# First stage of a two-layer trunk: modulation blocks loaded ahead of token groups 2 and 3, and the product groups put into another order

## The chip, the core and the metric

The kernel runs on one core of one Trainium2 chip. The metric is the device time of one execution in microseconds (us). Before the change, three runs took 1563.63, 1566.26 and 1572.01 us; the median is 1566.26 us.

## What is computed

The reference is one step of a two-layer trunk with 1024 latent tokens and 128 context tokens of width 1024. The change touches only the start of layer 0: the modulation, the pre-norm, and the key and value columns of the input product.

```python
def rms_norm(x, g):
    y = xf * lax.rsqrt(jnp.mean(xf * xf, axis=-1, keepdims=True) + EPS)
    return y * g
def adaln(cond, w, b):
    m = (jax.nn.silu(cond) @ w + b)[:, None, :]      # w: 1024 x 3072
    return split_last(m, (D_MODEL, D_MODEL, D_MODEL))  # shift, scale, gate
def pre_norm(x, g, mod):
    shift, scale, _ = mod
    return rms_norm(x, g) * (1 + scale) + shift
# even layer: q, k, v, ga, ub, gb = split(pre_norm(x) @ w_in); here only k and v (256 columns)
```

Everything behind it (attention, pooling, the second layer, the outputs) is as it was.

## The kernel before

The 1152 tokens are nine tiles of 128 (eight latent, the last one context), and each tile is loaded as 128 x 1024 (`xn`, 512 KB). Three tiles make a token group g = 0, 1, 2. The 1024 features are eight blocks k of 128.

A **product group** (k, g) is feature block k for token group g. Its work has two parts. `pn(k, g)` transposes the three normalised tiles on TensorE (three `tp` matmuls into one PSUM buffer), applies scale and shift on VectorE (`hf`; two instructions for g = 2, because the context tokens have other constants), rounds to the high part on ScalarE (`hTh`), and takes the low part on GpSimd (`hTl`). `kvg(k, ...)` then does nine matmuls of 128x256 (`kv`): high by high, low weights by high, high by low for three tiles. All 24 product groups add into five PSUM accumulators. The list `seq` is the order of the product groups, and `kvq(i)` does the matmuls of entry i.

The scale and shift of feature blocks 2b and 2b+1 come from **modulation block** b = 0 to 3. `mod_block_load(b)` loads four weight tiles `wmb` (512 KB each), `mod_block(b)` does 64 small matmuls into `modps` and copies the result out on VectorE (`mrow`), and `mod_block_end(b)` transposes it on TensorE and makes `sh` and `sc` with three short VectorE operations. So `pn(k, g)` needs the normalised tiles of g and modulation block k // 2.

Normalising a tile is a square-and-sum (`sqx`) and a square root (`xd`) on ScalarE, and a reciprocal (`xr`) and a scaling (`xn`) on VectorE. `norm_x` does the four in a row for one tile; `norm_x1` and `norm_x2` split them.

The weights of the k and v columns come in two halves (`raw`), each split into `whi` (ScalarE) and `wlo` (VectorE): `kv.load1(0)` and `kv.split1(0, ...)` for blocks 0 to 3, `kv.load1(1)` and `kv.split1(1, ...)` for blocks 4 to 7. `zeros(n)` are matmuls of zeros into the accumulators; they add nothing to a result and keep TensorE at work.

The order is written by hand: every engine works off its instructions in the order of the code, and an instruction that waits holds all behind it on its engine. All loads go through one queue on SyncE, in code order. The buffer for `hf` exists twice, and three PSUM buffers are left for `tp` and `modps` beside the accumulators. The 17 general slots of the pool that `wmb`, `raw`, `whi`, `wlo` and `zero` share are used in turn.

Names of lines: L115 every matmul, L124 every transpose, L131 ScalarE copies and casts (`hTh`, `whi`), L136 VectorE copies (`mrow`), L139 VectorE two-operand operations (`sh`, `sc`, `wlo`), L142 the same on GpSimd (`hTl`), L149 `xn`, L151 `hf`, L156 and L158 `xd` and `xr`, L337 and L589 `sqx`.

Of the kernel before, what the change touches and what calls it, by code (L numbers as in the profile page):

```python
# [566 lines left out]
def layer0(kn):  # L567
# [9 lines left out]
    def load_x(t):  # L577
        xn[t] = kn.S([128, 1024], name="xn")
        kn.dma(xn[t], xin(t))

    def norm_x(t):
        kn.xnorm(xn[t], kn.T([128, 1024], tag="sqx", bufs=1), xn[t])
# [3 lines left out]
    def norm_x1(t):  # L586

        ss = rx[t] = kn.T([128, 1], tag="xss3", bufs=3)
        nc.scalar.activation(out=kn.T([128, 1024], tag="sqx", bufs=1), in_=xn[t], func=AF.Square, accum_out=ss)  # L589

    def norm_x2(t):
        kn.vts(xn[t], xn[t], kn.rstd(rx[t], D, [128, 1], "x"))

    kv = Chunk(kn, w_in[:, 512:768], 256)
    mb = {}
# [4 lines left out]
    mb[0] = kn.mod_block_load(0)  # L600
    kv.load1(0)
    kn.setup1()
    for t in range(3, 6):
        load_x(t)
    mb[1] = kn.mod_block_load(1)
    for t in range(6, 9):
        load_x(t)
    kv.load1(1)

    hTh = [kn.S([128, 1152], F32R, name=f"hTh{k}") for k in range(8)]  # L610
    hTl = [kn.S([128, 1152], F32R, name=f"hTl{k}") for k in range(8)]
# [7 lines left out]
    def zeros(n, st=True, sp=True):  # L619
        for i in range(n):  # L620
            kn.mm(acc[i % 5], zero[:, 0:128], zero, st, sp)
# [4 lines left out]
    def pn(k, g, b=None):  # L626
        c = slice(384 * g, 384 * g + 384)
        kn.prenorm_k(0, g, k, xn[3 * g:3 * g + 3], hTh[k][:, c], hTl[k][:, c], b=b)

    def kvg(k, ts):  # L630
        for i in range(3):
            for t in ts:
                c = slice(128 * t, 128 * t + 128)
                last = i == 2 and k == 7 and (t == 8 or t % 2 == 1)
                kn.mm(kvps(t), (hTl if i == 2 else hTh)[k][:, c], (kv.lo if i == 1 else kv.hi)(k), False, last)


    seq = [(0, 0), (1, 0), (0, 1), (1, 1), (2, 0), (3, 0), (2, 1), (3, 1), (0, 2), (1, 2), (2, 2), (3, 2)]
    seq += [(k, g) for q in (4, 6) for g in range(3) for k in (q, q + 1)]
    kvq = lambda i: kvg(seq[i][0], range(3 * seq[i][1], 3 * seq[i][1] + 3))  # L640
    zeros(8)
    kn.setup()
# [11 lines left out]
    m = kn.mod_block(0, mb.pop(0))  # L654
    kn.mod_block_end(*m)
    zeros(10, False, False)
    kv.split1(0, True, 1)
    for t in range(3, 5):
        norm_x1(t)
    for k in range(2):  # L660
        pn(k, 0, tps[k])
    norm_x1(5)
    kv.split1(0, True, 2)
    mb[2] = kn.mod_block_load(2)
    for t in range(3, 6):
        norm_x2(t)
    for i in range(2):
        kvq(i)
    zeros(3, False, False)
    for i in range(2, 4):  # L670
        pn(*seq[i])
        zeros(3, False, False)
    for t in range(6, 9):
        norm_x(t)
    for i in range(2, 4):
        kvq(i)
    m = kn.mod_block(1, mb.pop(1))
    kn.mod_block_end(*m)
    for i in range(4, 7):
        pn(*seq[i])  # L680
    kv.split1(1, True)
    mb[3] = kn.mod_block_load(3)
    wl = Stream([Chunk(kn, w_in[:, 0:256], 256, veng=True), Chunk(kn, w_in[:, 256:512], 256, veng=True)])

    rt = {}
# [12 lines left out]
    kn.dma(cs[:, 1], I["k_sina"].rearrange("(t p) d -> p t d", p=128))  # L698
    kn.dma(nw[:, 2], I["cache_a_k"][0, 0])
    wl._load(0)  # L700
    for i in range(4, 24):
        if i in (8, 14):
            m = kn.mod_block(2 + i // 14, mb.pop(2 + i // 14))
        if i in (9, 15):
            kn.mod_block_end(*m)
        if i + 3 < 24:
            pn(*seq[i + 3])
        if i == 21:
            for c, w in rt.values():
                for x in range(2):  # L710
                    kn.ptt(c[:, x], cs[:, x], w[:, x, None, :].to_broadcast([128, 8, 64]))
        if i == 21:
            wl.need(0)
            wl._load(1)
        kvq(i)
# [1596 lines left out]
def body(nc, tc, I, O):  # L2312
    with ExitStack() as es:
        with tc.manual_schedule():
            kn = Kern(nc, tc, I, O, es)
            units, Qs, KHp, KLp, Vp = layer0(kn)
            attention_A(kn, units, Qs, KHp, KLp, Vp)
# [75 lines left out]
```

## Time and profile before

| what | value |
|---|---|
| median of three runs | 1566.26 us (1563.63 to 1572.01) |
| time of the profiled execution | 1571.76 us |
| its span | 1570.0 us |
| mean granted TensorE clock | 0.984 |
| TensorE busy | 1510.9 us (96%) |
| VectorE / ScalarE / GpSimd busy | 51% / 42% / 39% |
| last `kv` matmul begins | 67.96 us |

The profile comes from one execution, whose own time is 5.50 us over the median. TensorE is abbreviated PE (PEld is its weight load), VectorE DVE, ScalarE ACT, GpSimd POOL, SyncE SP. A row of the timeline gives start and length in us, the engine, line and operation, the tiles written and read, the count, and in square brackets the idle time before the instruction and what ended it. The rows of stretches give, for each engine, busy us in the stretch and instructions, then the granted clock (PEclk), the share of the DMA engines and GB/s.

### The profile page before, as it was taken

The page shows a single profiled execution, that of the slowest core. Times are in us where ns is not written, and L with a number is a line of the kernel's source. Part 1 is how long each engine was busy: PE and PEld are TensorE (multiplying, and loading weights), DVE is VectorE, ACT ScalarE, POOL GpSimd, SP SyncE. Part 2 cuts the span into 40 slices and gives each one's busy share as a digit, 9 for nine tenths or more (in the row PEclk, how much of TensorE's full clock was granted, in tenths as well). Part 3 has the DMA queues.
Part 4 walks back from the last instruction along what each step waited for, and adds up shares of the span by engine and source line. Part 5 has one row for each costly group of instructions (what it writes and reads, how often), then busy time and mean ns, then how long its engine had stood idle before and what let it go on. Part 6 is the DMA issues. An engine that isn't in the chain of part 4 may idle for free.

```text
span 1570.0 us, 23369 instructions
## 1 busy us (share of the span) xinstructions
PE 1510.9 (96%) x8957; PEld 1231.8 (78%) x8957; DVE 803.6 (51%) x1788; ACT 655.4 (42%) x1402; POOL 606.6 (39%) x508
## 2 busy tenths in 40 slices
PE   8998999999999999999999999999999999999998
PEld 6987998955545688998999999999866666665786
DVE  4575232466687655634353544423755555445643
ACT  5323212265645323444454545444454344345211
POOL 2652212069778224440313122001166566565221
PEclk9999999999999999999999999999999999899999
DMA  9343104120001232411304041050000000023241
GB/s 346 97 171 124 41 28 141 50 92 14 1 14 54 81 107 71 81 44 36 65 16 100 16 76 39 22 159 1 19 1 28 8 27 15 21 61 111 96 143 54
DMA packets 114079, 104.80 MB, mean 67 GB/s; under 512 B 41776, under 2 KB 99952, under 8 KB 113968
## 3 DMA queue, kind: packets, MB, share of 16 engines
q1 hardware_dynamic: 113792, 103.23, 22.1%
q8 instruction: 71, 1.16, 0.3%
q14 instruction: 40, 0.33, 0.1%
q10 hardware_dynamic: 176, 0.07, 0.0%
HBM read 87.54 MB, written 15.75 MB: 66 GB/s over the span
## 4 chain that ended last, share of the span: by engine, by line
PE 81%; DVE 9%; ACT 5%; DMA 2%; issue 2%; POOL 1%; SPq 0%; DVEq 0%; ACTq 0%; POOLq 0%
PE cg L115 14%; PE yps L115 12%; PE st L115 10%; PE gate L115 9%; PE pv L115 9%; PE lat L115 4%; PE mp L115 4%; PE cpv L115 3%; PE cS L115 2%; PE cT L124 2%; PE dq L115 2%; DVE mx L989 2%; DMA raw<-in_w_in_e 1%; PE kv L115 1%; PE dv L115 1%
## 5 line engine op out<-in xcount | busy, mean ns | idle before, releaser
L989 DVE TENSOR_REDUCE mx<-mp 128x1 f32<-128x384 f32 x384 | 190.1, 547 | 106.6 <-PE mp L115 105.3
L142 POOL TENSOR_TENSOR acc<-acc,P 128x1024 f32<-128x1024 f32 x84 | 200.6, 2388 | 67.4 <-ACT P L1029 64.5
L1029 ACT ACTIVATE P<-st 128x512 f32<-128x512 f32 x256 | 148.4, 598 | 151.4 <-PE st L115 137.3
L115 PE MATMUL yps<-whi,ohl 128*128 128x512 f32 x576 | 182.9, 393 | 0.0
L115 PE MATMUL cg<-hT1h,whi 128*128 128x384 f32 x480 | 169.2, 352 | 0.3 <-DVE hf L151 0.3
L115 PE MATMUL cg<-hT1h,wlo 128*128 128x384 f32 x480 | 161.9, 337 | 0.0
L115 PE MATMUL cg<-hT1l,whi 128*128 128x384 f32 x480 | 161.5, 337 | 0.0
L142 POOL TENSOR_TENSOR wlo<-raw,whi 128x1024 fp32r<-128x1024 f32 x25 | 60.0, 2400 | 245.8 <-ACT whi L131 174.4
L115 PEld LDWEIGHTS yps<-whi,ohl 128*128 128x128 f32 x576 | 108.1, 188 | 25.8 <-issue 3.7
L115 PE MATMUL yps<-wlo,ohl 128*128 128x512 f32 x288 | 112.2, 389 | 0.0
L115 PE MATMUL gate<-hTh,whi 128*128 128x384 f32 x288 | 98.9, 343 | 3.7 <-ACT whi L131 3.7
L115 PE MATMUL gate<-hTh,wlo 128*128 128x384 f32 x288 | 98.1, 340 | 0.3 <-DVE wlo L139 0.3
L115 PE MATMUL gate<-hTl,whi 128*128 128x384 f32 x288 | 97.6, 339 | 0.0
L115 PEld LDWEIGHTS cg<-hT1h,whi 128*128 128x128 f32 x480 | 90.5, 188 | 4.9 <-issue 3.4
L1638 ACT ACTIVATE cs<-cs,cnm 128x640 f32<-128x640 f32 (+1 forms) x64 | 54.8, 857 | 93.4 <-DVE cnm L149 92.7
L115 PEld LDWEIGHTS cg<-hT1l,whi 128*128 128x128 f32 x480 | 90.6, 189 | 0.5
L115 PEld LDWEIGHTS cg<-hT1h,wlo 128*128 128x128 f32 x480 | 90.1, 188 | 0.0
L139 DVE TENSOR_TENSOR wlo<-raw,whi 128x1024 fp32r<-128x1024 f32 (+2 forms) x35 | 46.6, 1340 | 65.3 <-ACT whi L131 64.6
L115 PE MATMUL pv<-P,dV 128*64 128x512 f32 x288 | 74.6, 646 | 1.7 <-DVE mx L989 1.7
L131 ACT CAST whi<-raw 128x1024 fp32r<-128x1024 f32 (+2 forms) x60 | 62.0, 1038 | 27.7 <-DMA raw<-in_w_in_e 13.5
L115 PE MATMUL st<-QH,dKh 96*128 96x512 f32 x144 | 63.5, 441 | 2.2 <-ACT P L1029 2.2
L115 PE MATMUL mp<-KH,QP 128*128 128x384 f32 x192 | 59.2, 365 | 6.4 <-DVE mx L989 3.5
(427 smaller groups left out, 3526.0 us busy)
## 6 DMA issues: line engine op xcount, KB each, us to landing
raw<-in_w_in_o SPq DMA_DIRECT2D x20, 512.0 KB, 4.1
raw<-in_w_in_e SPq DMA_DIRECT2D x18, 512.0 KB, 7.5
wmb<-in_w_mod SPq DMA_DIRECT2D x16, 512.0 KB, 8.5
wm<-in_w_mod SPq DMA_DIRECT2D x16, 512.0 KB, 7.4
wg<-in_w_mod SPq DMA_DIRECT2D x16, 512.0 KB, 5.2
x<-xr SPq DMA_DIRECT2D x9, 512.0 KB, 2.8
xr<-x SPq DMA_DIRECT2D x9, 512.0 KB, 4.6
xn<-in_x_sample SPq DMA_DIRECT2D x8, 512.0 KB, 7.1
```

Source lines behind the costliest of these rows:

```text
L115: self.nc.tensor.matmul(out=out, lhsT=l, rhs=r, start=st, stop=sp)
L124: self.nc.tensor.transpose(out, in_, self.ident[0:n, 0:n])
L131: self.nc.scalar.copy(out=out, in_=in_)
L139: self.nc.vector.tensor_tensor(out=out, in0=a, in1=b, op=op)
L142: self.nc.gpsimd.tensor_tensor(out=out, in0=a, in1=b, op=op)
L989: kn.nc.vector.tensor_reduce(out=self.mx[:, h, t, c:c + 1], in_=b, axis=AX.X, op=ALU.max)
L1029: kn.nc.scalar.activation(out=P[:, h], in_=a, func=AF.Exp, scale=self.scale)
L1638: nc.scalar.activation(out=s[:, 0:n], in_=s[:, 0:n], func=AF.Exp, bias=nm, accum_out=sm)
```

## The change

The loads are put in another order: modulation block 1 ahead of tiles 3 to 5, modulation block 2 and the second half of the k and v weights ahead of tiles 6 to 8, modulation block 3 last. The product groups are put in another order: blocks 0 to 3 of g = 0, blocks 0 to 3 of g = 1, then blocks 4 and 5 of both, then six blocks of g = 2, then blocks 6 and 7. Modulation block 1 is worked off right behind the first two product groups. The normalisation of tiles 3 to 5 is written behind it, and that of tiles 6 to 8 directly ahead of the first product group with g = 2. The count of matmuls for zeros goes from three times three in this stretch to three and six. Modulation blocks 2 and 3 are started by the loop when the next product group needs them.

```diff
     kn.setup1()
+    mb[1] = kn.mod_block_load(1)
     for t in range(3, 6):
         load_x(t)
-    mb[1] = kn.mod_block_load(1)
+    mb[2] = kn.mod_block_load(2)
+    kv.load1(1)
     for t in range(6, 9):
         load_x(t)
-    kv.load1(1)
...
-    seq = [(0, 0), (1, 0), (0, 1), (1, 1), (2, 0), (3, 0), (2, 1), (3, 1), (0, 2), (1, 2), (2, 2), (3, 2)]
-    seq += [(k, g) for q in (4, 6) for g in range(3) for k in (q, q + 1)]
+    seq = [(k, g) for g in range(2) for k in range(4)] + [(k, g) for g in range(2) for k in (4, 5)]
+    seq += [(k, 2) for k in range(6)] + [(k, g) for g in range(3) for k in (6, 7)]
...
-    for t in range(3, 5):
-        norm_x1(t)
     for k in range(2):
         pn(k, 0, tps[k])
-    norm_x1(5)
     kv.split1(0, True, 2)
-    mb[2] = kn.mod_block_load(2)
-    for t in range(3, 6):
-        norm_x2(t)
+    mb[3] = kn.mod_block_load(3)
     for i in range(2):
         kvq(i)
     zeros(3, False, False)
+    m = kn.mod_block(1, mb.pop(1))
+    kn.mod_block_end(*m)
+    zeros(6, False, False)
+    for t in range(3, 6):
+        norm_x1(t)
     for i in range(2, 4):
         pn(*seq[i])
-        zeros(3, False, False)
-    for t in range(6, 9):
-        norm_x(t)
-    for i in range(2, 4):
-        kvq(i)
-    m = kn.mod_block(1, mb.pop(1))
-    kn.mod_block_end(*m)
-    for i in range(4, 7):
-        pn(*seq[i])
-    kv.split1(1, True)
-    mb[3] = kn.mod_block_load(3)
+    for t in range(3, 6):
+        norm_x2(t)
+    pn(*seq[4])
...
-    for i in range(4, 24):
-        if i in (8, 14):
-            m = kn.mod_block(2 + i // 14, mb.pop(2 + i // 14))
-        if i in (9, 15):
+    done, m = 5, None
+    for i in range(2, 24):
+        if m:
             kn.mod_block_end(*m)
-        if i + 3 < 24:
-            pn(*seq[i + 3])
+            m = None
+        while done < min(24, i + 4):
+            k, g = seq[done]
+            if k in (4, 6) and g == 0 and k // 2 in mb:
+                m = kn.mod_block(k // 2, mb.pop(k // 2))
+                break
+            if (k, g) == (0, 2):
+                for t in range(6, 9):
+                    norm_x(t)
+            pn(k, g)
+            done += 1
+        if i == 5:
+            kv.split1(1, True)
         if i == 21:
```

How the two places stand on the engines, row by row, is shown here. **On PE, behind the first two product groups** (the `kv` rows are product groups, three rows each; `modps` from `wmb` is modulation block 1; `tp` are transposes, three to a product group), the order was:

```order
L115 MATMUL kv<-zero 128x512 x3
L124 MATMUL tp<-ident,xn 128x128 x3
L115 MATMUL kv<-zero 128x512 x3
L124 MATMUL tp<-ident,xn 128x128 x3
L115 MATMUL kv<-zero 128x512 x3
L115 MATMUL kv<-whi,hTh_122 128x256 x3
...
L115 MATMUL kv<-whi,hTl_131 128x256 x3
L115 MATMUL modps<-wmb,silrep 32x128 x32
L124 MATMUL modps<-ident,mrow 128x128
L124 MATMUL tp<-ident,xn 128x128 x12
L115 MATMUL kv<-whi,hTh_124 128x256 x3
```

and it is now:

```order
L115 MATMUL kv<-zero 128x512 x3
L115 MATMUL modps<-wmb,silrep 32x128 x32
L124 MATMUL modps<-ident,mrow 128x128
L115 MATMUL kv<-zero 128x512 x6
L124 MATMUL tp<-ident,xn 128x128 x12
L115 MATMUL kv<-whi,hTh_132 128x256 x3
L115 MATMUL kv<-wlo,hTh_132 128x256 x3
L115 MATMUL kv<-whi,hTl_140 128x256 x3
```

The twelve transposes belong to four product groups. Now they are (2, 0), (3, 0), (0, 1) and (1, 1), and the third to sixth product group stand behind all twelve.

**On ACT, around the normalisations of tiles 3 to 5 (L589) and 6 to 8 (L337)**, the rows of the change are these; the `hTh` rows are the product groups from (0, 0) on, `whi` is the second half of the k and v weights:

```order
L131 CAST hTh_131<-hf 128x384
L589 ACTIVATE sqx,xss_370<-xn 128x1024
L589 ACTIVATE sqx,xss_373<-xn 128x1024
L589 ACTIVATE sqx,xss_376<-xn 128x1024
L131 CAST hTh_132<-hf 128x384
L131 CAST hTh_133<-hf 128x384
L156 ACTIVATE xd<-xss_370,eps 128x1
...
L131 CAST whi<-raw 128x1024
L131 CAST hTh_134<-hf 128x384
L131 CAST hTh_135<-hf 128x384
L131 CAST hTh_134<-hf 128x384
L131 CAST hTh_135<-hf 128x384
L337 ACTIVATE sqx,xss<-xn 128x1024
L156 ACTIVATE xd<-xss,eps 128x1
```

In the kernel before, the square roots of tiles 3 to 5 stood right behind their squares, and the first L337 row of tiles 6 to 8 stood behind the fourth `hTh` row; now the square roots stand behind the fourth `hTh` row and that L337 row behind the twelfth.

**On PE, where token group 2 begins**, the change has:

```order
L115 MATMUL kv<-whi,hTh_134 128x256 x3
L115 MATMUL kv<-wlo,hTh_134 128x256 x3
L115 MATMUL kv<-whi,hTl_142 128x256 x3
L124 MATMUL tp<-ident,xn 128x128 x3
L115 MATMUL kv<-whi,hTh_135 128x256 x3
L115 MATMUL kv<-wlo,hTh_135 128x256 x3
L115 MATMUL kv<-whi,hTl_143 128x256 x3
```

The three transposes in the middle are those of (0, 2), the first that read tiles 6 to 8; they stand between the ninth product group and the tenth.

## The prediction

> **What bounds the kernel now.** I read the page's totals first, then stretches of the first stage, then the timeline of each engine inside it.
>
> ```profile
> span 1570.0 us, 23369 instructions
> PE 1510.9 (96%) x8957; PEld 1231.8 (78%) x8957; DVE 803.6 (51%) x1788; ACT 655.4 (42%) x1402; POOL 606.6 (39%) x508
> PE 81%; DVE 9%; ACT 5%; DMA 2%; issue 2%; POOL 1%; SPq 0%; DVEq 0%; ACTq 0%; POOLq 0%
> ```
>
> TensorE is the bound of the whole, and 81% of the chain that ended last. What the first stage gains or loses on PE moves the rest, because everything behind it needs its keys, values or `hTh`.
>
> ```profile
> 19.70:34.90 15.20, 12.07 (x128) 9.81 (x128) 9.62 (x21) 7.74 (x18) 4.51 (x4) 1.00 1.08 364
> 34.90:46.00 11.10, 10.22 (x126) 8.98 (x126) 6.23 (x14) 4.29 (x9) 6.97 (x7) 1.00 0.69 212
> 46.00:68.30 22.30, 22.10 (x236) 21.59 (x235) 11.53 (x25) 8.59 (x16) 14.72 (x14) 1.00 0.47 133
> ```
>
> In the third stretch PE is full (22.10 of 22.30 us): no order of the same matmuls makes it shorter. In the first it stands 3.13 us and in the second 0.88 us, while the DMA engines are full (1.08) up to 34.9. So only the work up to 46.00 us is open, and I follow PE there:
>
> ```profile
> 14.18 1.95 PE L115 MATMUL modps<-wmb,silrep 128*32 128x128 f32 x64
> 16.58 0.33 PE L124 MATMUL modps<-ident,mrow 128*128 128x128 f32 x1 [0.44 <-DVE mrow L136]
> 22.82 0.86 PE L115 MATMUL kv<-zero 128*128 128x512 f32 x3
> 23.51 0.49 PE L124 MATMUL tp<-ident,xn 128*128 128x128 f32 x2
> 28.97 1.95 PE L115 MATMUL modps<-wmb,silrep 128*32 128x128 f32 x64
> 32.76 0.33 PE L124 MATMUL modps<-ident,mrow 128*128 128x128 f32 x1 [1.83 <-DVE mrow L136]
> 46.00 0.60 PE L115 MATMUL kv<-whi,hTh 128*128 128x256 f32 x3
> 47.15 0.49 PE L124 MATMUL tp<-ident,xn 128*128 128x128 f32 x3
> 47.39 0.60 PE L115 MATMUL kv<-whi,hTh 128*128 128x256 f32 x3
> ```
>
> The largest stall is the 1.83 us ahead of 32.76: `mrow` was queued on DVE behind the normalisation of tiles 6 to 8. At 46.00 the tenth product group begins, and from there a product group with its transposes takes 47.39 - 46.00 = 1.39 us. The change has the same tenth-to-last work: 15 product groups, their transposes, modulation block 3. So the question is when the tenth product group begins: 46.00 us before, and now?
>
> **The change part by part: the loads.** Modulation block 1 goes ahead of tiles 3 to 5. Those now have 14 transfers of 512 KB ahead of the last of them (three tiles, four `wmb`, one `raw`, four `wmb`, two tiles). Before, tile 6 had 15 ahead of it:
>
> ```profile
> 17.30 9.98 DMA xn<-in_x_sample
> 27.30 1.06 ACT L337 ACTIVATE sqx<-xn 128x1024 f32<-128x1024 f32 x1
> 40.00:42.00 2.00, 1.76 (x11) 1.32 (x12) 1.09 (x4) 1.03 (x2) 1.33 (x2) 1.00 0.83 240
> 42.00:44.00 2.00, 2.00 (x67) 1.86 (x66) 1.46 (x4) 0.91 (x2) 1.44 (x2) 1.00 0.12 26
> ```
>
> Tile 6 was there by 17.30 + 9.98 = 27.28, so tile 5 now lands by 27.3 at the latest, and its square ends by 28.5. Modulation block 1 has 11 ahead of its last transfer and comes before tile 5. All 27 transfers are still the same, and the queue was drained by about 42 us (DMA share 0.83, then 0.12), which is the latest for tiles 6 to 8 and modulation blocks 2 and 3 too. Below, each is asked for later than that or lies well ahead in the queue: I cost the loads at nothing, and the cover ends if tile 5 lands after about 27.6.
>
> **The first wait that is added.** At 22.82 nothing differs yet. After the three zeros modulation block 1 takes the place of the transposes at 23.5. From its start to its transpose the row of block 0 gives 16.58 - 14.18 = 2.40 us, so 25.9, and six zeros at 0.23 us (23.51 - 22.82 for three) bring the twelve transposes to 27.5. The first six run, but the third set reads tiles 3 to 5, whose square roots now stand on ACT behind `hTh` of (2, 0) and (3, 0):
>
> ```profile
> 33.68 1.26 DVE L151 TENSOR_SCALAR hf<-tp,sc,sh 128x384 f32<-128x384 f32 x2
> 34.40 1.10 ACT L131 CAST hTh<-hf 128x384 fp32r<-128x384 f32 x2 [2.88 <-DVE hf L151]
> 21.04 0.80 ACT L156 ACTIVATE xd<-xss,eps 128x1 f32<-128x1 f32 x3
> 24.53 0.33 PE L124 MATMUL tp<-ident,xn 128*128 128x128 f32 x1 [0.53 <-DVE xn L149]
> 47.75 0.68 DVE L151 TENSOR_SCALAR hf<-tp,sc,sh 128x384 f32<-128x384 f32 x1 [0.55 <-PE tp L124]
> ```
>
> From a transpose to its `hf` it is 47.75 - 47.15 = 0.60 us, so `hf` begins at 28.1; two `hf` and two `hTh` take 34.40 + 1.10 - 33.68 = 1.82 us, to 29.9; and from the first square root to the last transpose that it frees, 24.53 - 21.04 = 3.49 us, to 33.4. With that transpose and the next set (0.4 us) the third product group starts at 33.8. PE stands from about 28.1 to 33.4, with four short transposes in it. Queued behind on PE are product groups three and four, whose `hTl` is ready by about 32: work that exists and may not run. Before, four product groups were done by then.
>
> From 33.8, three product groups with two sets of transposes take 3 x 1.39 - 0.3 = 3.9 us and modulation block 2 the 1.95 us of the row: it ends at M = 39.6.
>
> **The second wait.** The normalisation of tiles 6 to 8 stands on ACT behind `hTh` of the twelfth product group, and PE cannot pass the transposes of (0, 2) to the tenth product group. From M on, with these rows:
>
> ```profile
> 44.35 0.29 DVE L136 COPY mrow<-modps 128x128 f32<-128x128 f32 x1 [0.79 <-PE modps L115]
> 38.24 1.23 DVE L139 TENSOR_TENSOR wlo<-raw,whi 128x1024 fp32r<-128x1024 f32 x1 [1.53 <-ACT whi L131]
> 45.96 0.16 DVE L139 TENSOR_TENSOR sh<-modps,cols 128x4 f32<-128x4 f32 x1 [0.24 <-PE modps L124]
> 46.52 0.68 DVE L151 TENSOR_SCALAR hf<-tp,sc,sh 128x384 f32<-128x384 f32 x1
> 48.46 0.51 ACT L131 CAST hTh<-hf 128x384 fp32r<-128x384 f32 x1 [0.71 <-DVE hf L151]
> 49.05 1.01 POOL L142 TENSOR_TENSOR hTl<-hf,hTh 128x384 fp32r<-128x384 f32 x1 [0.22 <-ACT hTh L131]
> 41.73 1.83 DVE L151 TENSOR_SCALAR hf<-tp,sc,sh 128x256 f32<-128x256 f32 x4 [0.91 <-POOL hTl L142]
> 31.75 0.75 DVE L149 TENSOR_SCALAR xn<-xn,xr 128x1024 f32<-128x1024 f32 x1
> ```
>
> `mrow` ends at M + 0.4, `wlo` (now between it and `sh`) at M + 1.6, `sh` to `hf` takes 46.52 - 45.96 = 0.56, so `hf` of the ninth product group begins at M + 2.2, its `hTh` ends 1.2 us on (47.75 to 48.97) at M + 3.4, its `hTl` at M + 4.5 and that of the tenth at M + 5.5. The third `hf` from here must wait for the first `hTl` and the fourth for the second, because `hf` has two buffers (41.73 is such a wait): `hf` of the twelfth begins at M + 5.6, its `hTh` ends at M + 6.8. Then three tiles are normalised one behind another, before from 27.30 to 31.75 + 0.75 = 32.50, 5.2 us: M + 12.0. With the last transposes the tenth product group begins at M + 12.4 = 52.0. PE would have been there after five product groups and their transposes, at about M + 5.5: it stands 6 to 7 us. Queued behind are the tenth to twelfth product groups, all ready by M + 7.8.
>
> 52.0 against 46.00 is **+6.0 us**. The 1.83 us stall of before is gone in this sum; it is not gained, since the two new ones are longer.
>
> **The clock after the waits.** Before, these are the rows around two gaps of about 2 us:
>
> ```profile
> 30.00:32.00 2.00, 0.92 (x36) 0.65 (x24) 1.33 (x4) 1.48 (x4) 0.00 (x0) 1.00 1.10 349
> 96.48 0.44 PE L115 MATMUL qkv<-wlo,hTh 128*128 128x256 f32 x1 [1.99 <-DVE wlo L139]
> 96.00:98.00 2.00, 1.52 (x7) 1.52 (x8) 2.00 (x2) 0.00 (x0) 2.00 (x2) 0.67 0.26 33
> 98.00:100.00 2.00, 2.00 (x11) 2.00 (x11) 1.53 (x4) 0.78 (x2) 0.69 (x1) 0.50 0.91 356
> 154.00:156.00 2.00, 2.00 (x7) 2.00 (x8) 1.70 (x2) 1.55 (x2) 0.04 (x1) 0.50 0.48 137
> 156.00:158.00 2.00, 2.00 (x8) 2.00 (x7) 1.93 (x3) 0.00 (x0) 0.00 (x0) 0.50 0.77 213
> ```
>
> After the gap at 30.9 the clock stayed 1.00. After the 1.99 us before 96.48 it fell to 0.50: 1.52 us at 0.67 and 2 us at 0.50 lose 0.5 + 1.0 = 1.5 us, about 1.6 with the matmul's start. After a longer gap it was still 0.50 from 154 to 158, at least 2.0 us lost. Both new gaps are over twice 1.99 us, so I take a fall after each. Its price lies between 0 (as at 30.9) and about 2.5 us; I take the row at 96.48, 1.6 us, because there too PE goes on without a further wait. Both lie on the path: the first makes M later, and the second wait hangs on M. Two falls are **+3.2 us**.
>
> The page "TensorE: Matmul & The Clock Gate" of the Trainium skill (Part 1) says that the clock halves after at least one whole idle window of about 3.4 us and returns after about 3.4 us of work. The 0.50 after only 1.99 us here does not fit the first half; by that rule the first gap, broken by transposes, might pass free, and only the second would cost.
>
> **What is behind the stage.** `whi`, `wlo` and the first `sq` follow the last product groups in both orders with the same lead, so they move with PE. The next load that the path waits for, of `raw`, is issued at 144.51, straight behind a matmul of the chain:
>
> ```profile
> 136.39 8.12 PE gate L115 x47
> 144.51 6.87 DMA raw<-in_w_in_e
> ```
>
> So it moves too, and I give nothing back. The sum is 6.0 + 3.2 = 9.2 us. On the profiled execution's 1571.76 (span 1570.0 and 1.76 around it) that is 1581.0; this execution lies 5.5 above the median, so on the median it is 1566.26 + 9.2 = **1575.5 us**.
>
> **The rivals.** (A) Both waits come, but the clock falls at most once: +6.0 to +7.6, so 1572.3 to 1573.9. For it speaks the clock of 1.00 after 30.9, against it the length of the gaps. The skill's rule would give one fall: 1573.9.
>
> (B) The early block pays. If the last of tiles 3 to 5 were normalised by 28, ahead of `hTh` of (2, 0), the twelve transposes would end at 28.8, and the tenth product group could begin after seven more at 1.39 us and block 2: 28.8 + 9.7 + 2.0 = 40.5, 5.5 us ahead of 46.00, provided tiles 6 to 8 were also ready: 1560.8. That decides if no row on ACT stands between; the order on ACT speaks against it. A half of it, with only one wait left, ends near 1566.
>
> (C) The waits last longer: tiles land late (tile 5 after 27.6 adds its delay one for one), or each clock fall costs 2.5 us instead of 1.6: +11 to +13, so 1577 to 1579. For it speak the rows at 154 to 158.
>
> **How the numbers follow.** About 0.5%, 7.8 us, is what a measurement of this kernel can tell from no change; the bound lies at 1574.1. Forecast 0.50, (A) 0.27, (B) with its half 0.13, (C) 0.10. The three medians' own scatter (1563.6 to 1572.0) blurs the bound: of the forecast I count 0.75 as slower, of (A) 0.25, of (C) all: 0.375 + 0.07 + 0.10 = 0.55. Of (B) 0.04 is faster by over 0.5%. The rest, 0.41, is within. The range leaves out (B) and the tip of (C): 1567 to 1580. The forecast's own range with (C) is 1572 to 1580.
>
> **What would show it.** In the profile of the change: `modps` of block 1 at about 23.5 and its transpose at 25.9; PE idle from 28 with a wait for DVE `xn` ended near 33.4; a second wait for `xn`, 6 to 7 us, ahead of the tenth product group at 52 to 54; granted clock at 0.50 for about 3 us behind each; the last `kv` row near 77 instead of 67.96. If the transposes at 27.5 run through, the first step is wrong; if the tenth product group begins before 48, the second; if the clock stays 1.00, it is (A). If the last `kv` row is 9 us later and the time is not, something behind the stage gave it back.

## The result and the profile after

The changed kernel takes 1577.57 us (median of nine runs, 1574.65 to 1579.96), the kernel before beside it 1566.73 us (nine runs, 1563.57 to 1572.32). The ratio is 1.0053 with a 95% interval of 1.0037 to 1.0070: the change makes the kernel slower. The medians lie 10.8 us apart, and the interval of the ratio is 5.8 to 11.0 us of 1566.73. Forecast were 9.2 us more, on a median of 1566.26: 1575.5 us.

The profiled execution of the change took 1577.57 us, with a span of 1575.8 us. Of its first stage, this shows the stretch from 19.70 to 34.90 that was also shown of before, and then 2 us each in and behind the two waits (columns as before):

```profile
19.70:34.90 15.20, 9.45 (x106) 7.23 (x105) 6.87 (x14) 6.03 (x13) 4.90 (x4) 0.94 1.06 376
30.00:32.00 2.00, 0.00 (x0) 0.00 (x0) 1.19 (x3) 1.43 (x5) 1.68 (x2) 1.00 1.11 366
36.00:38.00 2.00, 2.00 (x12) 2.00 (x11) 0.50 (x1) 0.92 (x2) 1.52 (x2) 0.50 1.09 351
50.00:52.00 2.00, 0.00 (x0) 0.00 (x0) 0.57 (x2) 1.97 (x4) 1.07 (x2) 1.00 0.56 123
58.00:60.00 2.00, 2.00 (x11) 2.00 (x11) 0.86 (x2) 0.51 (x1) 0.46 (x2) 0.50 0.00 0
```

PE is busy 9.45 us of the 15.20 us where it was busy 12.07. It does nothing at all from 30 to 32 and from 50 to 52, and some us behind each of the two gaps it works at a granted clock of 0.50. In these two stretches ACT, DVE and POOL are at work.

The timeline of PE in the same profile:

```profile
6.82 0.20 PE L124 MATMUL col<-ident,crow 16*128 16x16 f32 x1 [1.58 <-DMA crow<-in_c_ctx]
24.47 1.95 PE L115 MATMUL modps<-wmb,silrep 128*32 128x128 f32 x64
26.87 0.33 PE L124 MATMUL modps<-ident,mrow 128*128 128x128 f32 x1 [0.44 <-DVE mrow L136]
28.43 0.82 PE L124 MATMUL tp<-ident,xn 128*128 128x128 f32 x6
32.97 0.30 PE L124 MATMUL tp<-ident,xn 128*128 128x128 f32 x1 [3.72 <-DVE xr L158]
33.74 0.48 PE L124 MATMUL tp<-ident,xn 128*128 128x128 f32 x1 [0.47 <-DVE xn L149]
34.60 1.11 PE L124 MATMUL tp<-ident,xn 128*128 128x128 f32 x4 [0.38 <-DVE xn L149]
35.36 0.99 PE L115 MATMUL kv<-whi,hTh 128*128 128x256 f32 x3
37.92 0.99 PE L115 MATMUL kv<-whi,hTh 128*128 128x256 f32 x3
40.26 0.60 PE L115 MATMUL kv<-whi,hTh 128*128 128x256 f32 x3
41.50 1.95 PE L115 MATMUL modps<-wmb,silrep 128*32 128x128 f32 x64
48.82 0.52 PE L115 MATMUL kv<-whi,hTl 128*128 128x256 f32 x3
52.49 0.30 PE L124 MATMUL tp<-ident,xn 128*128 128x128 f32 x1 [3.16 <-DVE xn L149]
53.77 0.48 PE L124 MATMUL tp<-ident,xn 128*128 128x128 f32 x1 [0.97 <-DVE xn L149]
55.13 0.48 PE L124 MATMUL tp<-ident,xn 128*128 128x128 f32 x1 [0.89 <-DVE xn L149]
55.26 0.99 PE L115 MATMUL kv<-whi,hTh 128*128 128x256 f32 x3
57.82 0.99 PE L115 MATMUL kv<-whi,hTh 128*128 128x256 f32 x3
60.38 0.66 PE L115 MATMUL kv<-whi,hTh 128*128 128x256 f32 x3
61.83 0.59 PE L115 MATMUL kv<-whi,hTh 128*128 128x256 f32 x3
79.13 0.52 PE L115 MATMUL kv<-whi,hTl 128*128 128x256 f32 x3
```

Two rows of the kernel before, to compare with the first and the last:

```profile
5.95 0.20 PE L124 MATMUL col<-ident,crow 16*128 16x16 f32 x1 [0.98 <-DMA crow<-in_c_ctx]
67.96 0.52 PE L115 MATMUL kv<-whi,hTl 128*128 128x256 f32 x3
```

The `col` row shows an offset: in this execution the first load that PE needs came 0.87 us later than in the profile of before (6.82 against 5.95), and all that follows stands 0.87 us later for that alone. The transposes of (0, 1) begin at 32.97 behind a wait of 3.72 us, and the third product group at 35.36. From the third to the fourth it is 2.56 us, to the fifth 2.34, where 1.39 is the pace at full clock. The second wait is 3.16, 0.97 and 0.89 us long, ahead of the tenth product group at 55.26, and behind it the steps are 2.56, 2.56 and 1.45 us. The last `kv` row stands at 79.13, and was at 67.96: 11.17 us, and 10.3 us without the offset.

What the two waits wait for stands on ACT and DVE of the same profile:

```profile
29.73 1.10 ACT L131 CAST hTh<-hf 128x384 fp32r<-128x384 f32 x2 [2.23 <-DVE hf L151]
30.74 0.81 ACT L156 ACTIVATE xd<-xss,eps 128x1 f32<-128x1 f32 x3
31.06 0.16 DVE L158 RECIPROCAL xr<-xd 128x1 f32<-128x1 f32 x1 [0.78 <-ACT xd L156]
49.47 0.51 ACT L131 CAST hTh<-hf 128x384 fp32r<-128x384 f32 x1 [0.46 <-DVE hf L151]
49.89 1.05 ACT L337 ACTIVATE sqx<-xn 128x1024 f32<-128x1024 f32 x1
```

The square roots of tiles 3 to 5 begin when `hTh` of (3, 0) is about done, and the square of tile 6 when `hTh` of the twelfth product group is about done.

The gap goes through the rest of the kernel, as the last matmuls of the group `lat` show (from the view by tile; the last two numbers ahead of the semicolon are the first and the last start; the first row is of before, the second of the change):

```profile
L115 PE MATMUL lat<-whi,hT1h x144: 311/317/417, 1046.9 to 1127.9; 128*128 128x336 f32 x144
```

```profile
L115 PE MATMUL lat<-whi,hT1h x144: 309/317/404, 1058.4 to 1139.1; 128*128 128x336 f32 x144
```

1139.1 - 1127.9 = 11.2 us, 10.3 without the offset. Behind that the two profiled executions come together again, to spans 5.8 us apart. The stretch from 1130 on, before and after:

```profile
1130.00:1500.00 370.00, 354.67 (x1671) 240.72 (x1670) 201.70 (x371) 163.37 (x323) 197.17 (x121) 0.96 0.15 44
```

```profile
1130.00:1500.00 370.00, 354.10 (x1714) 242.67 (x1713) 206.22 (x388) 166.83 (x341) 198.31 (x125) 0.98 0.14 43
```

The clock was 0.96 in the one execution and 0.98 in the other, and in the same 370 us the changed kernel did 1714 matmuls against 1671. That is a property of these two executions; the medians lie 10.8 us apart. It is taken up again in the last sections.

### The profile page after: what moved, and what is told of

Read it like the earlier page. It is cut to its first block, busy times and chain, and to the rows that moved or that the text cites. A ratio compares the mean times of both kernels' runs of the same rounds, so it can differ in the third digit from the quotient of the medians.

```text
span 1575.8 us, 23371 instructions
## 1 busy us (share of the span) xinstructions
PE 1510.2 (96%) x8957; PEld 1234.2 (78%) x8957; DVE 803.5 (51%) x1788; ACT 655.3 (42%) x1402; POOL 606.9 (39%) x508
## 4 chain that ended last, share of the span: by engine, by line
PE 81%; DVE 10%; ACT 5%; issue 2%; POOL 1%; DMA 1%; DVEq 0%; ACTq 0%; POOLq 0%
PE cg L115 14%; PE yps L115 12%; PE st L115 10%; PE gate L115 9%; PE pv L115 8%; PE lat L115 4%; PE mp L115 4%; PE cpv L115 3%; PE cS L115 2%; PE cT L124 2%; DVE mx L992 2%; PE dq L115 2%; PE kv L115 2%; PE dv L115 1%; PE tp L124 1%
## 5 line engine op out<-in xcount | busy, mean ns | idle before, releaser
L115 PE MATMUL st<-QH,dKh 96*128 96x512 f32 x144 | 62.2, 432 | 2.8 <-ACT P L1032 2.8
```

The costliest lines, as they stand in the source:

```text
L115: self.nc.tensor.matmul(out=out, lhsT=l, rhs=r, start=st, stop=sp)
```

## The experiments

The theory: two waits made by the order of work on ACT (the square roots of tiles 3 to 5 behind `hTh` of (3, 0), the normalisation of tiles 6 to 8 behind `hTh` of the twelfth product group), with a clock fall behind each. Against it stand three rivals: that the tiles come too late with the new loads; that the clock alone accounts for the loss; that what is lost in the stage is not what is lost in the time.

In the table, "stage" is the start of the last `kv` matmul (the third of the last row, from the view by tile), less the start of the `col` row, so that the offset of an execution drops out. It is read in one profiled execution of each kernel; the medians are of 4 to 12 executions. The kernel before ran beside each kernel on the same chip.

| kernel | stage, us | median, us | ratio to before, 95% interval |
|---|---|---|---|
| before | 62.2 | 1566.73 (9 runs) | |
| the change | 72.6 | 1577.57 | 1.0053 (1.0037 to 1.0070) |
| zeros in both waits | 69.3 | 1576.68 | 1.0062 (1.0040 to 1.0083) |
| zeros, all gaps | 67.7 | 1581.64 | 1.0077 (1.0051 to 1.0103) |
| roots first | 67.1 | 1571.40 | 1.0020 (1.0007 to 1.0034) |
| norms spread | 66.5 | 1571.93 | 1.0029 (1.0010 to 1.0047) |
| roots and norms | 64.2 | 1572.45 | 1.0029 (1.0010 to 1.0048) |
| loads alone | 68.8 | 1572.15 | 1.0041 (1.0026 to 1.0056) |
| order alone | 71.7 | 1576.57 | 1.0063 (1.0040 to 1.0086) |
| another order from before | 63.7 | 1573.61 | 1.0029 (1.0012 to 1.0046) |
| before, 10 us of zeros | 72.3 | 1578.73 | 1.0061 (1.0040 to 1.0082) |
| before, 5 us of zeros | 66.6 | 1579.49 | 1.0063 (1.0038 to 1.0088) |

The kernel before had medians of 1568.66 us (25 runs) beside zeros in both waits, roots first, norms spread, and roots and norms; 1566.84 us (24 runs) beside zeros in all gaps, loads alone, order alone, and another order; and 1567.96 us (11 runs) beside the last two.

### Which part makes the wait: roots first

```diff
         norm_x1(t)
-    for i in range(2, 4):
-        pn(*seq[i])
     for t in range(3, 6):
         norm_x2(t)
+    for i in range(2, 4):
+        pn(*seq[i])
     pn(*seq[4])
```

> The changed kernel with the square roots and scalings of tiles 3 to 5 ahead of pn of (2, 0) and (3, 0), nothing else. Theory: the square roots follow the last square at 27.4 instead of hTh of (3, 0) at 30.7, the transposes of (0, 1) run by about 31 instead of 35, but hf of (2, 0) now stands behind three scalings, so the third product group begins at about 32 instead of 35.4: 3 us earlier, and 2.1 us more if the shorter gap keeps the clock: last kv row 74 to 76, time 3 to 5 us under the change. Rival (the tiles come too late because of the new order of the loads, and the order on ScalarE does not matter): the transposes of (0, 1) stay near 33 to 35 and the time stays within 1 us of the change.

PE in this kernel, timeline:

```profile
29.13 0.33 PE L124 MATMUL tp<-ident,xn 128*128 128x128 f32 x1 [0.23 <-DVE xn L149]
29.99 0.33 PE L124 MATMUL tp<-ident,xn 128*128 128x128 f32 x1 [0.53 <-DVE xn L149]
31.12 0.62 PE L115 MATMUL kv<-whi,hTh 128*128 128x256 f32 x3
33.72 0.52 PE L115 MATMUL kv<-whi,hTl 128*128 128x256 f32 x3
46.56 0.30 PE L124 MATMUL tp<-ident,xn 128*128 128x128 f32 x1 [3.18 <-DVE xn L149]
```

The wait of 3.72 us is one of 0.23 and 0.53, the third product group begins at 31.12 instead of 35.36 (3.5 us earlier without the offset), and the fourth ends at the pace of the full clock. The second wait stands as it was, 3.18 us. The stage is 5.5 us shorter, a little more than expected, and the median 6.2 us under that of the change. So the place of the second half of the normalisation made the first wait. The edit moves two things, the square roots on ACT and the scalings on DVE. In the change DVE was done with the two `hf` at 30.28 and idled only 0.78 us for the first root, so earlier roots alone, with the scalings still behind the two `hf`, would have saved about 0.8 us of the wait (an estimate from these rows; it was not run).

### Norms spread, and both edits

The second edit, alone:

```diff
-            if (k, g) == (0, 2):
-                for t in range(6, 9):
-                    norm_x(t)
             pn(k, g)
+            if done in (6, 7, 9):
+                norm_x({6: 6, 7: 7, 9: 8}[done])
             done += 1
```

> The changed kernel with tile 6 normalised behind pn of the seventh product group, tile 7 behind the eighth and tile 8 behind the tenth, instead of all three ahead of pn of (0, 2); the loads are those of the change. Theory: the second wait (5.9 us from the end of the ninth product group to the tenth) and the clock fall behind it (2.4 us) go: last kv row at about 71, time about 8 us under the change, 1569 to 1570. Rival (tiles 6 to 8 land too late, behind block 2 and the second weight half): sqx of tile 6 to 8 waits for its DMA beyond 42 and the wait of TensorE only moves: less than 3 us saved.

The stage was 6.1 us shorter, not 8.3: the wait of 3.16 us ahead of (0, 2) was down to 0.74, but there was a new one of 1.04 us for `mrow` of modulation block 2; the clock stayed at full pace behind both. The median was 5.6 us under that of the change.

> Both edits of the two runs before together, with the loads and the order of product groups of the change. Theory: the two savings add up, 11 to 13 us: last kv row 66 to 68, time 1564 to 1567, level with the kernel before; the new order of loads and product groups in itself would then cost and gain next to nothing. Rival (the load order or the product order costs something itself): 3 us or more over the kernel before.

With both edits the stage is 8.4 us shorter, where 11 to 13 us were expected. The first and second wait are gone and a third has come, seen on PE and on DVE of this kernel:

```profile
42.27 0.33 PE L124 MATMUL modps<-ident,mrow 128*128 128x128 f32 x1 [3.12 <-DVE mrow L136]
41.06 0.16 DVE L158 RECIPROCAL xr<-xd 128x1 f32<-128x1 f32 x1 [1.96 <-ACT xd L156]
41.92 0.28 DVE L136 COPY mrow<-modps 128x128 f32<-128x128 f32 x1
```

The result of block 2 was there when its matmuls ended near 37.9, but its copy stands on DVE behind the scaling of tile 7, which waits for ACT. It is the same wait as the 1.83 us of the kernel before, at another block. Behind it the clock fell once more: the next product groups begin at 43.00, 44.99 and 47.34, which is 1.6 us more than two steps of 1.39. My sum of the two savings left out that the normalisation has to stand somewhere: it went from in front of a transpose to in front of `mrow`. The stage ends 2.0 us behind that of before, so neither the theory (level with before) nor the rival (3 us or more over) holds exactly by the stage; by the median, 3.8 us over the 1568.66 us beside it, the rival's bound is passed, which the stage does not account for.

### The loads and the order, each alone

The kernel before with the loads in the new order:

```diff
     kn.setup1()
+    mb[1] = kn.mod_block_load(1)
     for t in range(3, 6):
         load_x(t)
-    mb[1] = kn.mod_block_load(1)
+    mb[2] = kn.mod_block_load(2)
+    kv.load1(1)
     for t in range(6, 9):
         load_x(t)
-    kv.load1(1)
```

(the load of modulation block 3 is moved up to where that of block 2 stood)

> The kernel before with the loads in the order of the change (modulation block 1 ahead of tiles 3 to 5, block 2 and the second weight half ahead of tiles 6 to 8), the order on all other engines as before. Theory (the new order of the work makes the waits, and the loads are only its condition): here the loads cost in another way, because the squares of tiles 3 and 4 stand on ScalarE ahead of the first hTh and now wait for tiles that land near 23.7 and 25.0 instead of 16.8 and 18.1, and the normalisation of tiles 6 to 8 stands ahead of mrow of block 1 on VectorE and waits for tiles that land at 36 to 39: last kv row 75 to 78, time 7 to 10 us over the kernel before. Rival (the loads are free, they are only queued otherwise): within 2 us of the kernel before.

The stage is 6.6 us longer than that of before (last `kv` matmul at 74.9), the median 5.3 us over it: the direction of the theory, and a little less than it had expected. PE waits twice:

```profile
26.23 1.01 PE L115 MATMUL kv<-whi,hTh 128*128 128x256 f32 x3 [5.96 <-ACT hTh L131]
40.10 0.33 PE L124 MATMUL modps<-ident,mrow 128*128 128x128 f32 x1 [2.28 <-DVE mrow L136]
```

So the new loads need a new order of the work: with the old one ACT stands behind late tiles. Behind each of the two waits the clock fell too: `kv` rows take 0.84 us there instead of 0.52.

And the changed kernel with the loads of before (the first hunk of the diff above the other way round, and blocks 2 and 3 loaded where the kernel before loaded them):

> The changed kernel with the loads in the order of the kernel before; the order on the other engines is that of the change. Theory: both waits are made by the order on ScalarE, so both stay although tiles 3 to 8 are there earlier; modulation block 1 now lands near 26, where TensorE already stands at 23.6, so the first part is 1 to 3 us later still: last kv row 80 to 82, time 0 to 3 us over the change. Rival (the change loses because tiles 3 to 8 come later): last kv row 70 or less, time within 2 us of the kernel before.

```profile
33.39 0.30 PE L124 MATMUL tp<-ident,xn 128*128 128x128 f32 x1 [3.71 <-DVE xr L158]
35.79 0.99 PE L115 MATMUL kv<-whi,hTh 128*128 128x256 f32 x3
38.15 0.60 PE L115 MATMUL kv<-whi,hTh 128*128 128x256 f32 x3
51.78 0.45 PE L124 MATMUL tp<-ident,xn 128*128 128x128 f32 x1 [3.17 <-DVE xn L149]
```

Here tiles 3 to 8 come as early as before, and the two waits are the same to 0.01 us: 3.71 and 3.17 against 3.72 and 3.16. That rules out the rival that the tiles come late. The transpose of modulation block 1 stood at 27.30, 1.0 us later, net of the offset, than with the new loads, as expected. The last `kv` matmul still came at 78.0, 2 us ahead of what I had expected, because both clock falls were shorter here. From the third to the fifth product group it took 3.74 us (2.36 and 1.38) instead of 4.90 in the change, and the steps behind the second wait held 1.8 us of loss instead of 2.4. So the same wait does not cost the same fall each time.

### The clock: zeros in the waits

```diff
         pn(*seq[i])
+    zeros(14, False, False)
     for t in range(3, 6):
...
             if (k, g) == (0, 2):
+                zeros(13, False, False)
                 for t in range(6, 9):
```

> The changed kernel with 14 matmuls of zeros put between the transposes of (3, 0) and (0, 1), and 13 ahead of the transposes of (0, 2): they fill most of both waits on TensorE (3.72 us and 3.16 us at 0.23 us each) and end before the data are there, so neither wait gets shorter. Theory (two waits made by the order on ScalarE, and a clock fall behind each): the clock stays 1.00 behind both, the product groups behind them take 1.39 us instead of 2.56, and the 2.1 + 2.4 us of the two falls are saved: last kv row at about 74.6 instead of 79.13, time about 1573 (4.5 us under the change). Rival 1 (the clock accounts for nearly all, the waits would be hidden): last kv row near 68 to 70. Rival 2 (the clock costs nothing on the path): last kv row stays at 79, time the same.

> As the first run with zeros, and five matmuls of zeros more between the transposes of tiles 6 and 7, and of 7 and 8, in the second wait, whose gaps of 0.98 and 1.04 us were left open there and let the clock fall to 0.50 from 52 to 57. Theory: with these gaps filled the clock stays 1.00 in the whole stage, and 1.4 us more are saved than with the first run: last kv row at 74.5 to 75 (76.2 there, 79.4 in the change), start of the last seen at the same offset of 6.9. Rival (the clock falls whatever is filled in): last kv row at 76.

(the second of the two adds five matmuls of zeros behind the first and behind the second transpose of (0, 2))

Stretches behind the second wait, of the change, of the first kernel with zeros, and of the second:

```profile
54.00:58.00 4.00, 3.11 (x15) 2.87 (x15) 1.78 (x4) 0.61 (x2) 0.79 (x1) 0.50 0.78 256
```

```profile
54.00:58.00 4.00, 4.00 (x25) 4.00 (x24) 1.39 (x4) 1.02 (x2) 2.02 (x2) 0.63 0.80 261
```

```profile
54.00:58.00 4.00, 4.00 (x37) 4.00 (x37) 2.46 (x6) 1.48 (x3) 3.02 (x3) 1.00 0.61 207
```

With most of the waits filled, the clock stayed at 1.00 behind the first, though gaps of 0.59, 0.47 and 0.53 us were left there, and still fell behind the second, to 0.63 in this stretch, where gaps of 0.21, 0.98 and 1.04 us were left ahead of the transposes; the stage was 3.3 us shorter than that of the change, not 4.5. With those gaps filled too the clock stayed at 1.00 and the stage was 4.9 us shorter: 4.5 in the steps of the product groups and 0.4 in the last transposes of the first wait (below). The transposes behind the waits came no earlier. So the falls cost 4.9 us in the stage, and the other 5.5 of the 10.4 us between the stages of before and after are the waits themselves, net of those of before that are gone. That the clock accounts for nearly all is out, and so is that it costs nothing on the path of the stage.

The medians did not follow. The first of these kernels is 0.9 us under the change, where 4.5 were expected, the second 4.1 us over it, though its stage ends 4.9 us earlier. The next section takes this up.

### Is a delay of the stage carried to the end?

The kernel before with a pure delay, without idle time and without a clock fall in the stage:

```diff
+        if i == 10:
+            zeros(44, False, False)
         if i + 3 < 24:
             pn(*seq[i + 3])
```

> The kernel before with 44 matmuls of zeros (0.235 us each) ahead of the eleventh product group, where TensorE is full and the other engines are ahead: a pure delay of 10.3 us of everything behind, with no idle time and no clock fall in the first stage. It is the delay that the change showed at the end of the stage. Theory (a delay of the first stage is carried to the end one for one): last kv row 78.3 to 78.6 instead of 68.2, last matmul of the lat group 10.3 us later than 1127.9, median 9 to 11 us over the kernel before. Rival (something behind the stage gives a part back, or the clock falls further on depend on when they come and outweigh it): median less than 7 or more than 13 us over.

> The same with 22 matmuls of zeros, a delay of 5.2 us. Theory: last kv row 73.1 to 73.5, median 4 to 6 us over the kernel before, half of the run with 44. Rival (the time behind the stage depends on when it begins): the medians of the two runs are not in the ratio of 1 to 2; this one lies less than 3 or more than 8 us over the kernel before.

The longer delay lengthened the stage by 10.1 us and the median by 10.8 us (1578.73 against 1567.96), as expected. The shorter one lengthened the stage by 4.4 us and the median by 11.5 us (1579.49): the rival's result. The last matmul of `lat` stood at 1139.2 after the longer delay and at 1133.7 after the shorter one, 11.1 and 5.4 us later than before without the offset. In all eleven profiles of other kernels it lies within 2.5 us of where the difference of the stages puts it. So the stage is carried to there, but what lies behind is not the same after each delay. The stretch that follows the `lat` group, in the profile of the longer delay and in that of the shorter one:

```profile
1130.00:1300.00 170.00, 161.05 (x801) 113.71 (x800) 95.04 (x198) 80.53 (x175) 93.77 (x62) 0.98 0.07 19
```

```profile
1130.00:1300.00 170.00, 159.99 (x761) 112.60 (x760) 90.50 (x182) 77.88 (x164) 92.19 (x58) 0.94 0.07 19
```

The same instructions behind the stage, 0.98 against 0.94 of the clock, 801 against 761 matmuls in 170 us. And within one kernel the time follows the mean granted clock of the execution: the kernel before took 1563.41 us at 0.990 and 1571.78 us at 0.983, the kernel with all gaps filled 1569.90 us at 0.991 and 1584.21 us at 0.982.

An estimate parts the two. The time of each execution times its mean granted clock is what it would take without a loss of clock; the rest is the loss. The means over the executions of a kernel are:

| kernel | time x clock, us | loss, us |
|---|---|---|
| before (60 runs beside the experiments) | 1548.0 | 20.1 |
| the change | 1552.7 | 24.2 |
| before, 10 us of zeros | 1558.8 | 19.4 |
| before, 5 us of zeros | 1553.3 | 25.3 |
| zeros, all gaps | 1555.3 | 24.2 |

By the first column the two delays cost 10.8 and 5.3 us, near the 10.1 and 4.4 us of their stages, and the change 4.7 us, near the 5.5 us of its waits; the 4.1 us that it loses more to the clock are near the 4.9 us of its two falls. The filled gaps fit less well, 7.3 us for a stage 5.5 us longer. The shorter delay and the filled gaps have no fall in the stage and still lose 4 to 5 us more clock than the kernel before, so that loss lies behind the stage. It is why the medians do not follow the stages; what makes it larger in one kernel than in another was not found.

### A version that keeps the loads of before

```diff
+    m = kn.mod_block(1, mb.pop(1))
+    norm_x(6)
+    kvq(2)
+    kn.mod_block_end(*m)
+    for i in range(4, 6):
+        pn(*seq[i])
+    kvq(3)
+    norm_x(7)
+    pn(*seq[6])
+    norm_x(8)
-    for t in range(6, 9):
-        norm_x(t)
-    for i in range(2, 4):
-        kvq(i)
-    m = kn.mod_block(1, mb.pop(1))
-    kn.mod_block_end(*m)
-    for i in range(4, 7):
-        pn(*seq[i])
```

> The kernel before, loads and product order as they were, with modulation block 1 and its sh and sc ahead of the scaling of tiles 7 and 8, and tiles 6, 7, 8 normalised one at a time between product groups instead of three in a row ahead of mrow. Theory: the 1.83 us wait for mrow at 32.76 and part of the 0.88 us of PE idle time up to 46 go; the fifth product group begins at 31 to 33 instead of 34.96: last kv row 65 to 66 instead of 67.96, time 2 to 3 us under the kernel before. Rival (another wait takes its place: tile 8 now comes too late for (0, 2), or block 2 is not there): last kv row 67 to 69, no difference.

The wait of 1.83 us for `mrow` went, and the fifth product group began at 32.27 instead of 34.96. But tile 8 was then late for (0, 2):

```profile
38.45 0.47 PE L124 MATMUL tp<-ident,xn 128*128 128x128 f32 x1 [3.17 <-DVE xn L149]
```

The clock fell with it: the granted clock was 0.50 from 36 to 42. The stage ended 1.5 us later than before. The rival had named the place, but not the time: it expected no difference, and the median lay 6.8 us over that of before. None of the kernels run here beats the kernel before.

## Why the prediction was right

**The first wait.** Forecast: modulation block 1 at 23.5, its transpose at 25.9, the third product group at 33.8. Measured, less the offset of 0.87: 23.6, 26.0 and 34.5. The cause was as given, the place of the normalisation behind `hTh` of (3, 0), and the run with the roots first shows it, for roots and scalings together. The 0.7 us that were missing lie in two places. One half is the scaling of tile 3, here beside `hTl` on POOL:

```profile
31.26 1.56 DVE L149 TENSOR_SCALAR xn<-xn,xr 128x1024 f32<-128x1024 f32 x1
```

It took 1.56 us, and I had taken over the 1.22 of the kernel before with the row at 24.53; that the work on POOL makes it longer is likely, since alone it takes 0.75, but was not tested. The other half is the fallen clock: from the last transposes to the third product group it took 0.76 us (34.60 to 35.36) instead of the 0.4 that I had allowed. In the first run with zeros it took 0.41:

```profile
34.71 0.66 PE L124 MATMUL tp<-ident,xn 128*128 128x128 f32 x4 [0.53 <-DVE xn L149]
35.12 0.60 PE L115 MATMUL kv<-whi,hTh 128*128 128x256 f32 x3
```

**The second wait.** Forecast: the tenth product group at M + 12.4. Measured: the matmuls of modulation block 2 end at 41.50 + 1.95 = 43.45, and the tenth product group begins at 55.26, M + 11.8. The chain that I had put together row by row was 0.6 us too long. PE was through with the ninth product group at 49.3, M + 5.9, after four product groups behind M; the prediction says five, a miscount, but its M + 5.5 is the sum of four.

**The loads.** Costed at nothing, and right: with the loads of before both waits keep their length, and modulation block 1 is done 1.0 us later. Tile 5's square began at 26.35 in this profile, so it landed ahead of the 27.3 that I had taken as its bound.

**The clock.** Two falls came. The step that was too small is this term: 3.2 us forecast, 2.1 us (2.56 + 2.34 - 2 x 1.39 = 2.12) and 2.4 us (2.56 + 2.56 + 1.45 - 3 x 1.39) measured by the steps of the product groups, 4.5 together, and 4.9 by filling the gaps, with the 0.4 us of the transposes. I had taken the price of the row at 96.48; the higher bound of 2.5 us was the nearer one. The page "TensorE: Matmul & The Clock Gate" of the Trainium skill (Part 1) has the clock halve after an idle window of about 3.4 us. The prediction drew from it that the first gap might pass and the second not. In the trace it is the first wait that has 3.72 us without a break, long enough for such a window, while the second has no gap over 3.16 us, and the clock fell behind both; with zeros in the second wait, gaps of 0.21, 0.98 and 1.04 us were enough. The measurement decides.

**The sum.** 9.2 us forecast for the stage, 10.3 measured: + 0.3 for the first wait, + 1.7 for the clock (4.9 instead of 3.2), - 0.6 for the second wait, - 0.3 for the rest of the stage. That the sum is only 1.1 us off is in part luck, as errors of both signs cancel. Rival (A), one fall at most, is refuted by the two stretches at 0.50. Rival (B) did not come, and the run with both edits shows that even without the two waits the stage would not have ended 5 us earlier than before, since the third wait takes their place. The part of (C) on the price of the clock came true, and the 1577.57 us lie in its 1577 to 1579; its late tiles did not come.

**What is behind the stage.** I gave nothing back, and the 10.3 us at `lat` and the run with the 10 us delay agree. But the step was argued only as far as the next load. In the median a delay of 4.4 us cost 11.5 us, and a stage shorter by 4.9 us gave a median longer by 4.1. So a median that lies 10.8 us over that of before is in line with the 10.3 us of the stage, and does not prove them to a microsecond: kernels with 5 us less or half the delay in the stage have medians as high. That the median came so near is in part luck; what a delay does to the later clock falls is not settled.

## What to carry to other kernels

In an order written by hand, ask of each load that is brought forward what the *order of work* behind it now holds up: an instruction of ScalarE or VectorE that stands too late holds up all that TensorE has queued behind it, and moving it in front of something else can move the wait there, in part or whole, as in three of the runs here (norms spread, roots and norms, another order from before). Price an idle gap of TensorE with the gap itself and with the slow us behind it, which cost almost as much as the gaps here. And judge a change of a few us in an early stage by where the stage ends in the trace as well as by the median, as the median takes in clock falls further on, whose length differs between executions of one kernel and which the stage does not account for.

## What was not expected of the hardware

The clock falls further on in the program are not of one length from execution to execution. In the stretch from 1130 to 1300 the mean granted clock was 0.97 in the profile of the kernel before, 0.99 in that of the change, 0.98 and 0.94 in those of the two delays, for the same program behind the stage; the time of the whole execution follows (1563.41 us at 0.990, 1571.78 us at 0.983 for the kernel before). A pure delay of the first stage of 4.4 us moved the median by 11.5 us and one of 10.1 us by 10.8 us. What decides the length of a fall was not found; the runs show that it is not the work alone. Nor does the same wait bring the same fall: waits of 3.72 and 3.16 us were followed by a loss of 2.1 and 2.4 us in the steps of the change, waits of 3.71 and 3.17 us by 1.0 and 1.8 us with the loads of before. A fall does not need one long gap: behind 0.98 and 1.04 us with one transpose between, the clock was 0.63 on average from 54 to 58, and with the gaps filled it stayed at 1.00; gaps of 0.59, 0.47 and 0.53 us in the first wait of the same kernel brought none.
